# A decode convolution buffer with time outermost, and a decode z projection from the block in SBUF

## The chip, the cores and the metric

The kernel runs on one core of one Trainium2 chip. The metric is the device time of one execution in microseconds (us); it is the median of several runs. A profile is one more execution, taken by the hardware profiler; its span runs from the first to the last instruction.

## What is computed

The reference is one inference step of a one-layer hybrid trunk. A prompt of 2048 tokens and a decode batch of 8 sequences of 4 tokens (32 rows) share all weights. Each group goes through an input LayerNorm, a modulation of every channel by a vector `c`, one input projection, two mixers side by side (a state space branch and attention in a window of 128 with sinks), an output projection, a normalised residual, a squared-ReLU feed-forward part, and a second normalised residual. The state space branch is where the change lies:

```python
def causal_conv(u, buf, w, b):
    t = u.shape[1]
    up = jnp.concatenate([buf.astype(u.dtype), u], 1)
    y = up[:, 0:t] * w[0]
    for j in range(1, CONV_W):
        y = y + up[:, j:j + t] * w[j]
    return jax.nn.silu(y + b), up[:, t:]
...
    z = p[..., :Z_END]
    xbc = p[..., Z_END:XBC_END]
...
    y = y.reshape(b, t, SSM_WIDTH) * jax.nn.silu(z.astype(jnp.float32))
```

For the decode rows `buf` is `state_conv`, the last three positions of 1024 channels of each of the 8 sequences; the new state, the last three of the seven positions, is an output. The convolution has four taps. `z`, 512 channels, gates the branch's output.

## The kernel before

Everything is float32. A matmul whose operands must be exact is done as three: both operands are split into a high and a low part (`float32r`), and high x high, high x low and low x high are summed in PSUM (`mm3`, lines 164 to 167). The 32 decode rows have a cheaper way, `mm_dec` (lines 149 to 155): the high and low parts of the 32 rows stand side by side as 64 stationary columns, two matmuls for each block of 128 channels make 64 rows of partial sums in PSUM, ScalarE copies these to SBUF, and `sum2` (lines 157 and 158) adds the upper and the lower 32 rows by a matmul with a matrix of ones and zeros.

The work runs in sweeps. Sweep 1 makes step sizes, q, k, v and the attention of 16 token tiles of 128 and one decode tile, and stores the modulated input, split and transposed, in DRAM (`hT_d`). Sweep 2, which the change touches, goes over the tokens in 8 blocks of 256 (the loop at line 948). Block `BD` = 2 carries the decode tile as well, as columns 256 to 288 of its `hT`. For each block:

- `ld_hT` (line 632) brings in a block of `hT`, one block ahead. Even blocks use the buffers `hTa0` and `hTa1`, of which there is one each, so block 4's four loads (line 643) can only start when block 2's `hT` has been read for the last time. At block 2 two more loads (line 646) bring in the decode columns, high and low.
- `xproj` (line 654) makes the 8 groups of 128 convolution channels: 24 matmuls each into one of three PSUM tiles `mm`, an eviction by ScalarE (line 673), the convolution on VectorE (`conv4`, line 649: one instruction of line 650 and three of line 652), and a SiLU on ScalarE (line 679). At block 2 each group has 32 more columns, which VectorE copies from PSUM into the decode buffer `xd` (line 677) and convolves in the same way (line 678).
- `zproj` (line 826) makes `z` of a token tile; `zproj(2, 2)` makes that of the decode rows, by `mm_dec` and `sum2`. It loads its operand `hz` (line 833) from `hT_d` and puts `hz` and the copied partial sums into the rings of the tiles `X` and `Xd`.
- `ssd1` and `ssd2` (lines 844 and 904) do the scan of one chunk of 128 tokens. `ssd1` loads the running sums of the decays, broadcast to all partitions (`csb`, line 849), turns them into a masked decay matrix (VectorE line 863, ScalarE line 864, VectorE line 875), and makes `X` (line 865) and, on GpSimd, `Xd` (line 867). `ssd2` has PE's lines 913, 917 and 923, ends in VectorE's line 938, and stores its result to `yn_d` (line 939). `dec_half` does the decode part with the stored states.

The decode buffer `xd` is one SBUF tile. Its state part is loaded at the start of sweep 2 (line 822), and its last three positions are stored after `zproj(2, 2)` (line 969):

```python
xd = p2.tile([128, 8, 8, 7], F32, name="xd")
D.dma_start(out=xd[:, :, :, 0:3], in_=I["sconv"])
...
D.dma_start(out=O["convs"], in_=xd[:, :, :, 4:7])
```

The dimensions are channel in its group (partition), group, sequence, time. The DRAM sides, `sconv` and `convs`, have 192 contiguous values for each partition.

In this part of the kernel the order of the instructions on each engine comes from the compiler's scheduler: each engine runs its own list in order, and program order is the priority. Loads and stores named `D` are issued by SyncE (SP), one after the other, on one DMA queue; a DMA that has to wait for its buffer holds up those behind it on SP.

After sweep 2 come the output projection with the first residual (line 999 on) and the feed-forward part (from line 1197), which takes more than half of the time. Neither is touched.

Of the kernel before, what the change touches and what calls it, by code (L numbers as in the profile page):

```python
# [10 lines left out]
F32 = mybir.dt.float32  # L11
F32R = mybir.dt.float32r
# [8 lines left out]
ND = NB * NT_  # L21
NTOK = T + ND
DM, DFF = 1024, 4096
NTILE = T // 128
# [47 lines left out]
def host_arrays(i):  # L72
    a = {}
    f = lambda n: np.asarray(i[n])
    a["consts"], a["dmask"] = host_consts()
    a["x"] = np.concatenate([f("x_prompt")[0], f("x_sample").reshape(ND, DM)], 0)
    c = np.concatenate([f("c_prompt"), f("c_sample")], 0)
    a["cT"] = c.T.reshape(8, 128, 9).transpose(1, 0, 2)
    wa = f("w_ada")[0].reshape(8, 128, 6144)
    wc = wa[:, :, :2048].reshape(2, 4, 128, 2, 8, 128)[:, :, :, ::-1].transpose(4, 0, 2, 1, 3, 5)  # L80
    a["w_ac"] = wc.reshape(8, 2, 128, 1024)
    a["w_ada"] = wa[:, :, 2048:].reshape(8, 128, 8, 512).transpose(2, 1, 0, 3)
    col = lambda v: v.reshape(-1, 128).T
    a["acol"] = np.concatenate([col(f("b_ada")[0, :2048]), col(f("ln_in_g")), col(f("ln_in_b"))], 1)
    a["b_ada"] = f("b_ada")
    w = f("w_in")[0].reshape(8, 128, 2312)
    a["w1"] = w[:, :, 1536:2312]
    a["wx"] = w[:, :, 512:1536]
    a["wz"] = w[:, :, 0:512]
    cw = f("conv_w")[0].reshape(4, 8, 128).transpose(2, 1, 0)  # L90
    cb = f("conv_b")[0].reshape(8, 128).T[:, :, None]
    a["conv"] = np.concatenate([cw, cb], 2)
    a["sconv"] = f("state_conv")[0].reshape(8, 3, 8, 128).transpose(3, 2, 0, 1)
    h = 4 * np.arange(2)[:, None] + np.array(HR)[None, :]
    a["small"] = np.concatenate(
        [f("dt_bias"), f("A_log"), f("D_skip"), f("sinks")[:, h.reshape(-1)],
         f("sinks")], 0)
    a["normw"] = f("ssm_norm_w")
    a["rows"] = np.stack([f("ln_in_g"), f("ln_in_b"), f("ln1_g")[0], f("ln1_b")[0], f("ln2_g")[0], f("ln2_b")[0]], 0)
    wo = f("w_out")[0]  # L100
    att = wo[512:].reshape(2, 4, 64, 1024)[:, HR].transpose(1, 0, 2, 3).reshape(4, 128, 1024)
    a["wo"] = np.concatenate([wo[:512].reshape(4, 128, 1024), att], 0)
    a["wu"] = f("w_up")[0].reshape(8, 128, 32, 128).transpose(2, 1, 0, 3)
    a["wd"] = f("w_down")[0].reshape(32, 128, 1024)
    a["h0"] = f("state_ssm")[0].reshape(8, 512, 128).transpose(0, 2, 1)
    ck, cv = f("cache_k")[0], f("cache_v")[0]
    a["ckT"] = ck.transpose(3, 2, 0, 1).reshape(64, 2, 1024)
    a["ck"] = ck.reshape(8, 128, 128)
    a["cv"] = cv.reshape(8, 128, 128)
    return {k: np.ascontiguousarray(v) for k, v in a.items()}  # L110
# [1 line left out]

OUTS = {
    "y": (NTOK, DM), "convp": (128, 8, 3), "ssmp": (128, 512), "kp": (128, 128), "vp": (128, 128),
    "convs": (128, 8, 8, 3), "ssms": (8, 128, 512), "ks": (8, 128, 128), "vs": (8, 128, 128),
}


def body(tc, I, O):
    nc = tc.nc  # L120
    V, S, G, PE, D = nc.vector, nc.scalar, nc.gpsimd, nc.tensor, nc.sync
# [23 lines left out]
    ud_d = tc.dram_tile([2 * ND, DM], F32, name="ud_d")  # L145
    h2_d = tc.dram_tile([9, 128, 2, 8, 128], F32, name="h2_d")

# [1 line left out]
    def mm_dec(tmp, w, hs, wt):  # L149
        acc = mm_tile()  # L150
        for k in range(8):
            for l in range(2):
                PE.matmul(acc[:2 * ND, :w], lhsT=hs(k), rhs=wt(k, l), start=k + l == 0, stop=k + l == 8)
        S.activation(tmp[:2 * ND, :w], acc[:2 * ND, :w], AF.Copy)
        return tmp

    def sum2(out, tmp, w):
        PE.matmul(out[:ND, :w], lhsT=idt[:2 * ND, 192:224], rhs=tmp[:2 * ND, :w], start=True, stop=True)
# [5 lines left out]
    def mm3(out, ahi, alo, bhi, blo, first=True, last=True):  # L164
        PE.matmul(out, lhsT=ahi, rhs=bhi, start=first, stop=False)  # L165
        PE.matmul(out, lhsT=ahi, rhs=blo, start=False, stop=False)  # L166
        PE.matmul(out, lhsT=alo, rhs=bhi, start=False, stop=last)  # L167
# [18 lines left out]
    def ptok(t):  # L186
        return 128 if t < NTILE else ND

# [1 line left out]
    cp = pool("const")  # L190
    mhalf = cp.tile([128, 2], F32, name="mhalf")
    V.memset(mhalf, -0.5)
# [18 lines left out]
    dt_all = cs_.tile([128, NC, 8], F32, name="dt_all")  # L211
    V.memset(dt_all, 0.0)

# [1 line left out]
    pk = pool("dk")  # L215
    dk = {}
    for nm in ("cs", "ecs", "dst", "etot"):
# [58 lines left out]
        if ch < 7:  # L276
            ada_ld(ch + 1)

# [1 line left out]
    p1 = pool("sweep1")  # L280
    W1h = [page(k)[:, 0:776] for k in range(8)]
    W1l = [page(8 + k)[:, 0:776] for k in range(8)]
# [252 lines left out]
            D.dma_start(out=att_d[NTILE][:, :, :32], in_=ao)  # L535
            dec["p"].release()

# [1 line left out]
    def decays_a():  # L539
        cs, ecs, dst, etot = dk["cs"], dk["ecs"], dk["dst"], dk["etot"]  # L540
        bc = lambda a: a.unsqueeze(1).to_broadcast([128, NC, 8])
# [51 lines left out]
        D.dma_start(out=cs_d[0:128, :], in_=cT_[:, 0:128])  # L593
        D.dma_start(out=cs_d[128:136, 0:32], in_=cT_[:8, 128:160])

# [1 line left out]
    NA = 4  # L597
    Wx, Wz = {}, {}
    w2 = {}
# [49 lines left out]
    def conv4(dst_, src, f):  # L649
        V.tensor_scalar(dst_, src(0), cvw[:, f, 0:1], cvw[:, f, 4:5], ALU.mult, ALU.add)  # L650
        for j in range(1, 4):
            V.scalar_tensor_tensor(dst_, src(j), cvw[:, f, j:j + 1], dst_, ALU.mult, ALU.add)  # L652

    def xproj(b, fs):
        N = 256 if b != BD else 288
        hT = blk["hT", b]
        if fs[0] == 0:
            p, tg = (pb, "xcb") if b % 2 else (pb, "xca")
            blk["xc", b] = p.tile([128, 8, 256 if b % 2 else 288], F32, tag=tg, name="xc")
            blk["halo", b] = xq[:, 800 + 24 * (b % 2):824 + 24 * (b % 2)].rearrange("p (f t) -> p f t", t=3)  # L660
        xc, halo = blk["xc", b], blk["halo", b]
        for f in fs:
            o = 260 * ((8 * b + f) % 3)
            xp = xq[:, o:o + 259]
            if b == 0:
                V.memset(xp[:, 0:3], 0.0)
            else:
                V.tensor_copy(xp[:, 0:3], blk["halo", b - 1][:, f, :])
            mm = mm_tile()
            cs4 = slice(128 * f, 128 * f + 128)  # L670
            for k in range(8):
                mm3(mm[:, :N], Wx[k][0][:, cs4], Wx[k][1][:, cs4], hT[0][:, k, :N], hT[1][:, k, :N], k == 0, k == 7)
            S.activation(xp[:, 3:259], mm[:, 0:256], AF.Copy)
            V.tensor_copy(halo[:, f, :], xp[:, 256:259])
            conv4(xc[:, f, 0:256], lambda j: xp[:, j:j + 256], f)
            if N > 256:
                V.tensor_copy(xd[:, f, :, 3:7], mm[:, 256:288].rearrange("p (b t) -> p b t", b=8))
                conv4(xc[:, f, 256:288].rearrange("p (b t) -> p b t", b=8), lambda j: xd[:, f, :, j:j + 4], f)
            S.activation(xc[:, f, :N], xc[:, f, :N], AF.Silu)

    extras = [] + [lambda ch=ch: ada_step(ch) for ch in range(8)]
# [69 lines left out]
    for i in range(n + 3):  # L751
# [3 lines left out]
        t = g(i)  # L755
# [57 lines left out]
        extras.pop(0)()  # L813
    p1.release()

# [1 line left out]
    p2 = pool("sweep2")  # L817
    cs, ecs, dst, etot, etb = [dk[k] for k in ("cs", "ecs", "dst", "etot", "etb")]
    St = [p2.tile([128, 512], F32, name=f"St{j}") for j in range(2)]
    V.memset(St[0], 0.0)  # L820
    xd = p2.tile([128, 8, 8, 7], F32, name="xd")
    D.dma_start(out=xd[:, :, :, 0:3], in_=I["sconv"])
    hbc = lambda a, P: a.unsqueeze(2).to_broadcast([P, 8, 64])
    h3 = lambda a: a.rearrange("p (h d) -> p h d", h=8)

    def zproj(b, m):
        P = 128 if m < 2 else 32
        hT = blk["hT", b]
        mm = mm_tile()
        sl = slice(128 * m, 128 * m + P)  # L830
        if m == 2:
            hz = p2.tile([128, 8, 2 * ND], F32R, tag="X", name="hz", bufs=2)
            D.dma_start(out=hz.bitcast(F32), in_=hT_d[NTILE][:, 0, :, :2 * ND])
            tmp = mm_dec(p2.tile([128, 512], F32, tag="Xd", name="tmp", bufs=2), 512, lambda k: hz[:, k, :],
                         lambda k, l: Wz[k][l])
            sum2(mm, tmp, 512)
        else:
            for k in range(8):
                mm3(mm[:P, :], hT[0][:, k, sl], hT[1][:, k, sl], Wz[k][0], Wz[k][1], k == 0, k == 7)
        z = p2.tile([128, 512], F32, tag="z", name="z", bufs=3)  # L840
        S.activation(z[:P], mm[:P, :], AF.Silu)
        blk["z", 2 * b + m if m < 2 else NTILE] = z
# [105 lines left out]
    for b in range(7):  # L948
        ld_hT(b + 1)
        if b > 0:  # L950
            xproj(b, range(0, 4))
        if b > 0:
            ssd2(2 * b - 2)
            ssd1(2 * b - 1)
        if b == BD + 1:
            ssd1(NTILE)
        if b > 0:
            xproj(b, range(4, 8))
            ssd2(2 * b - 1)
        if b == BD + 1:  # L960
            dec_half(0)
        zproj(b, 0)
        ssd1(2 * b)
        if b == BD + 1:
            dec_half(1)
        zproj(b, 1)
        if b == BD:
            zproj(b, 2)
            D.dma_start(out=O["convs"], in_=xd[:, :, :, 4:7])
        if b == BD + 1:  # L970
            ssd2(NTILE)
    xproj(7, range(0, 4))
# [23 lines left out]
    S.dma_start(out=O["convp"], in_=blk["halo", 7])  # L996
    S.dma_start(out=O["ssmp"], in_=St[NTILE % 2])

# [1 line left out]
    first2 = {}  # L1000

    def q2(nm, dt_=F32):
# [191 lines left out]
    pw.release()  # L1194
    out_c(NTILE - 1)

# [1 line left out]
    p4 = pool("ffn")  # L1198
    T4 = {"st": (3, F32), "st2": (1, F32), "wvh": (1, F32R), "wvl": (1, F32R),
          "r": (2, F32), "gf": (1, F32), "wdh": (3, F32R), "wdl": (3, F32R)}  # L1200
# [329 lines left out]
```

## Time and profile before

| | |
|---|---|
| runs | 2547.44, 2553.53, 2552.56 us; median 2552.56 us |
| span of the profiled execution | 2549.4 us, 32193 instructions |
| mean granted PE clock | 0.976 |
| PE matmul busy | 2429.9 us (95%) |
| VectorE (DVE) busy | 1502.2 us (59%) |
| ScalarE (ACT) busy | 717.9 us (28%) |
| GpSimd (POOL) busy | 933.2 us (37%) |
| DMA | 133672 packets, 244.46 MB; 43408 packets under 512 B |

A row of a timeline is start, duration (us), engine, line of the kernel, operation, tile written <- tiles read, shapes and how many were merged; in brackets stands how long the engine had been idle before it, and what released it. SPq rows are DMA issues by SyncE: their duration is the time to issue, not to transfer. A row of waits is engine, tile and line, what it waited for, and then the total in us, the number of times and the longest. A row of windows is a stretch, its length, busy time of PE, PE's weight loads, DVE, ACT and POOL (with numbers of instructions), the granted PE clock, the mean busy share of the 16 DMA engines, and GB/s. Rows of a tile are number, minimum/median/maximum duration in ns, first and last start, and shapes.

### The profile page before, as it was taken

The numbers are of one execution on the slowest core, as the hardware profiler recorded it, in microseconds if no ns is written. First come the engines' busy times: TensorE is split into PE (matmuls) and PEld (weight loads), VectorE is DVE, ScalarE is ACT, GpSimd is POOL, SyncE is SP. The second block draws the span as 40 slices with busy tenths as digits, with TensorE's granted clock in tenths as the row PEclk, the third lists the DMA queues.
The fourth block names the chain that finished last, engine by engine and source line by source line (L and its number), as shares of the span: only waits on it lengthen the run. The fifth ranks groups of instructions, "written<-read, shape, count | busy, mean of one in ns | idle before, by whom it ended". The sixth has DMA issues, their size and how long they took to land.

```text
span 2549.4 us, 32193 instructions
## 1 busy us (share of the span) xinstructions
PE 2429.9 (95%) x12688; PEld 2013.2 (79%) x12688; DVE 1502.2 (59%) x2582; ACT 717.9 (28%) x1433; POOL 933.2 (37%) x602
## 2 busy tenths in 40 slices
PE   8999998959999998899999999999899999999997
PEld 6667787947997877687888888888788988988985
DVE  6756666837879888764544434447844344344347
ACT  3544474312434222312212121212221221221221
POOL 4323431213323454544333233435532332332335
PEclk9999999979999999999999999999899999999998
DMA  8644433483225435621111111117311110110111
GB/s 319 247 172 158 133 106 90 64 55 109 83 67 194 141 116 192 217 62 60 60 42 58 46 58 42 51 49 205 121 44 48 34 67 34 42 58 34 42 43 72
DMA packets 133672, 244.46 MB, mean 96 GB/s; under 512 B 43408, under 2 KB 78416, under 8 KB 130368
## 3 DMA queue, kind: packets, MB, share of 16 engines
q1 hardware_dynamic: 129120, 232.42, 29.5%
q10 hardware_dynamic: 4400, 9.98, 1.1%
q8 instruction: 100, 1.64, 0.3%
q14 instruction: 52, 0.43, 0.1%
HBM read 188.00 MB, written 55.37 MB: 95 GB/s over the span
## 4 chain that ended last, share of the span: by engine, by line
PE 52%; DVE 3%; issue 1%; POOL 1%; ACT 0%; POOLq 0%; DVEq 0%
PE sc L165 10%; PE sc L167 10%; PE sc L166 10%; PE mm L165 5%; PE mm L167 5%; PE mm L166 5%; PE tr L167 2%; PE tr L166 2%; PE tr L165 2%; PE tr L1282 1%; DVE p L1237 1%; DVE p L1294 0%; DVE nb L1306 0%; POOL rs L173 0%; DVE p L1313 0%
## 5 line engine op out<-in xcount | busy, mean ns | idle before, releaser
L162 POOL TENSOR_TENSOR wdl<-st,wdh 128x1024 fp32r<-128x1024 f32 x63 | 164.2, 2606 | 533.1 <-ACT wdh L161 533.1
L1267 DVE TENSOR_TENSOR r<-r 128x320 f32<-128x320 f32 (+1 forms) x160 | 148.4, 928 | 300.7 <-ACT u L1263 101.2
L1294 DVE TENSOR_TENSOR p<-mm,p 128x512 f32<-128x512 f32 x298 | 202.6, 686 | 175.6 <-PE mm L167 175.5
L161 ACT ACTIVATE wdh<-st 128x1024 fp32r<-128x1024 f32 x63 | 66.8, 1060 | 628.7 <-PE mm L167 244.9
L165 PE MATMUL sc<-H,wvh 128*128 128x352 f32 (+1 forms) x640 | 227.7, 356 | 5.9 <-ACT r L1261 5.9
L167 PE MATMUL sc<-H,wvl 128*128 128x352 f32 (+1 forms) x640 | 226.6, 354 | 0.0
L166 PE MATMUL sc<-H,wvh 128*128 128x352 f32 (+1 forms) x640 | 226.3, 354 | 0.0
L165 PE MATMUL sc<-H,wuh 128*128 128x352 f32 (+1 forms) x640 | 224.7, 351 | 0.0
L167 PE MATMUL sc<-H,wul 128*128 128x352 f32 (+1 forms) x640 | 224.0, 350 | 0.0
L166 PE MATMUL sc<-H,wuh 128*128 128x352 f32 (+1 forms) x640 | 223.9, 350 | 0.0
L1261 ACT ACTIVATE r<-sc 128x352 f32<-128x352 f32 (+1 forms) x160 | 81.7, 511 | 273.8 <-PE sc L167 237.0
L165 PEld LDWEIGHTS sc<-H,wvh 128*128 128x128 f32 x640 | 121.3, 189 | 18.8 <-ACT r L1261 6.2
L166 PEld LDWEIGHTS sc<-H,wvh 128*128 128x128 f32 x640 | 121.2, 189 | 12.0
L167 PEld LDWEIGHTS sc<-H,wvl 128*128 128x128 f32 x640 | 120.8, 189 | 12.2
L165 PEld LDWEIGHTS sc<-H,wuh 128*128 128x128 f32 x640 | 120.5, 188 | 11.5 <-ACT r L1261 0.8
L167 PEld LDWEIGHTS sc<-H,wul 128*128 128x128 f32 x640 | 121.0, 189 | 10.5
L166 PEld LDWEIGHTS sc<-H,wuh 128*128 128x128 f32 x640 | 120.7, 189 | 10.2
L173 POOL TENSOR_TENSOR rs<-ve,mhalf 128x1 f32<-128x1 f32 (+2 forms) x68 | 48.6, 715 | 207.7 <-DVE ve L172 186.2
L1143 DVE TENSOR_TENSOR st<-st,gf 128x1024 f32<-128x1024 f32 x64 | 84.7, 1323 | 56.3 <-POOL wdl L162 46.9
L1294 DVE TENSOR_TENSOR p<-tr,p 128x512 f32<-128x512 f32 x102 | 69.8, 687 | 75.3 <-PE tr L167 75.3
L1266 DVE TENSOR_TENSOR ud<-r 128x32 f32<-128x32 f32 x32 | 58.3, 1822 | 94.8 <-ACT r L1261 94.8
L652 DVE SCALAR_TENSOR_TENSOR xc<-xq,cvw,xc 128x256 f32<-128x256 f32 x192 | 103.2, 541 | 2.8
(487 smaller groups left out, 6635.2 us busy)
## 6 DMA issues: line engine op xcount, KB each, us to landing
st<-in_wd SPq DMA_DIRECT2D x64, 512.0 KB
st<-in_wu SPq DMA_DIRECT2D x63, 512.0 KB
wa<-in_w_ada SPq DMA_DIRECT2D x32, 512.0 KB
hT_d<-hb SPq DMA_DIRECT2D x16, 1024.0 KB
hT<-hT_d SPq DMA_DIRECT2D x16, 512.0 KB
hT<-hT_d SPq DMA_DIRECT2D x8, 1024.0 KB
csb<-cs_d SPq DMA_DIRECT2D x16, 512.0 KB
p<-xhat_d SPq DMA_DIRECT2D x16, 512.0 KB
```

The costliest lines, as they stand in the source:

```text
L161: S.activation(hi, src, AF.Copy)
L162: (eng or V).tensor_tensor(lo, src, hi.bitcast(F32), ALU.subtract)
L165: PE.matmul(out, lhsT=ahi, rhs=bhi, start=first, stop=False)
L166: PE.matmul(out, lhsT=ahi, rhs=blo, start=False, stop=False)
L167: PE.matmul(out, lhsT=alo, rhs=bhi, start=False, stop=last)
L173: G.tensor_tensor(r[:P], v[:P], mhalf[:P, 0:n], ALU.pow)
L652: V.scalar_tensor_tensor(dst_, src(j), cvw[:, f, j:j + 1], dst_, ALU.mult, ALU.add)
L1143: V.tensor_tensor(st, raw, scale, ALU.mult)
L1261: S.activation(r[:, :n], mm[:, :n], AF.Relu)
L1266: V.tensor_tensor(ud, r[:, w:n], r[:, w:n], ALU.mult)
L1267: V.tensor_tensor(r[:, :w], r[:, :w], r[:, :w], ALU.mult)
L1294: V.tensor_tensor(acc[t][:, sl], mm, acc[t][:, sl], ALU.add)
```

## The change

The decode buffer `xd` is laid out as partition, time, group, sequence, and the DRAM arrays `sconv` and `convs` with it. So the state part is the first 3 x 64 values of each partition and the new state the last 3 x 64: both are contiguous on both sides. The host's arrangement of input and output changes to match. VectorE's copy from PSUM and its convolution get views in which time stands before sequence. `zproj(2, 2)` no longer loads `hz` and no longer uses `mm_dec` and `sum2`; it is done like the others, with `mm3`, from columns 256 to 288 of the block's `hT` in SBUF, 32 rows at a time. The rest of the diff is comments removed.

```diff
-    a["sconv"] = f("state_conv")[0].reshape(8, 3, 8, 128).transpose(3, 2, 0, 1)
+    a["sconv"] = f("state_conv")[0].reshape(8, 3, 8, 128).transpose(3, 1, 2, 0)
...
-    "convs": (128, 8, 8, 3), "ssms": (8, 128, 512), "ks": (8, 128, 128), "vs": (8, 128, 128),
+    "convs": (128, 3, 8, 8), "ssms": (8, 128, 512), "ks": (8, 128, 128), "vs": (8, 128, 128),
...
-                V.tensor_copy(xd[:, f, :, 3:7], mm[:, 256:288].rearrange("p (b t) -> p b t", b=8))
-                conv4(xc[:, f, 256:288].rearrange("p (b t) -> p b t", b=8), lambda j: xd[:, f, :, j:j + 4], f)
+                tb = lambda a: a.rearrange("p (b t) -> p t b", b=8)
+                V.tensor_copy(xd[:, 3:7, f, :], tb(mm[:, 256:288]))
+                conv4(tb(xc[:, f, 256:288]), lambda j: xd[:, j:j + 4, f, :], f)
...
-    xd = p2.tile([128, 8, 8, 7], F32, name="xd")
-    D.dma_start(out=xd[:, :, :, 0:3], in_=I["sconv"])
+    xd = p2.tile([128, 7, 8, 8], F32, name="xd")
+    D.dma_start(out=xd[:, 0:3], in_=I["sconv"])
...
-        if m == 2:
-            hz = p2.tile([128, 8, 2 * ND], F32R, tag="X", name="hz", bufs=2)
-            D.dma_start(out=hz.bitcast(F32), in_=hT_d[NTILE][:, 0, :, :2 * ND])
-            tmp = mm_dec(p2.tile([128, 512], F32, tag="Xd", name="tmp", bufs=2), 512, lambda k: hz[:, k, :],
-                         lambda k, l: Wz[k][l])
-            sum2(mm, tmp, 512)
-        else:
-            for k in range(8):
-                mm3(mm[:P, :], hT[0][:, k, sl], hT[1][:, k, sl], Wz[k][0], Wz[k][1], k == 0, k == 7)
+        for k in range(8):
+            mm3(mm[:P, :], hT[0][:, k, sl], hT[1][:, k, sl], Wz[k][0], Wz[k][1], k == 0, k == 7)
...
-            D.dma_start(out=O["convs"], in_=xd[:, :, :, 4:7])
+            D.dma_start(out=O["convs"], in_=xd[:, 4:7])
...
-        np.ascontiguousarray(o["convs"].transpose(2, 3, 1, 0)).reshape(1, 8, 3, 1024),
+        np.ascontiguousarray(o["convs"].transpose(3, 1, 2, 0)).reshape(1, 8, 3, 1024),
```

## The prediction

> **What bounds the kernel now.** I read the page first, then the waits of TensorE (PE), then the timeline around the longest of them, then the DMA view of the same stretch. On the page PE is busy in nine tenths or more of nearly every slice:
>
> ```profile
> span 2549.4 us, 32193 instructions
> ...
> PE   8999998959999998899999999999899999999997
> ```
>
> So time can only be won where PE is made to stand still. Slice 9 (510 to 573 us) has a 5 in the middle of the state space sweep. The waits of PE between 400 and 700 us (engine, its line, what it waited for: total us, times, longest) name the cause:
>
> ```profile
> PE mm L153 <- DMA hz<-hT_d: 28.0, 1, 28.0
> PE sc L923 <- DVE csb L875: 1.8, 1, 1.8
> ...
> PE mm L165 <- ACT xq L673: 0.8, 1, 0.8
> ```
>
> One wait of 28.0 us is for the operand `hz` of the decode z projection, the second thing that the change touches. The timeline (start, duration, engine, line, what; in brackets the idle time before it and its releaser) shows that `hz` is not what is slow:
>
> ```profile
> 498.15 0.59 SPq L969 DMA_DIRECT2D out_convs<-xd  x1
> ...
> 498.88 21.80 SPq L849 DMA_DIRECT2D csb<-cs_d  x1
> ...
> 503.85 1.46 DVE L652 SCALAR_TENSOR_TENSOR xc<-xd,cvw,xc 128x32 f32<-128x32 f32 x2
> ...
> 511.51 1.02 PE L913 MATMUL sc<-St,xc 128*128 128x256 f32 x4
> 520.73 2.20 SPq L833 DMA_DIRECT2D hz<-hT_d  x1
> 539.65 1.66 DVE L863 TENSOR_SCALAR csb<-csb,dk_cs 128x128 f32<-128x128 f32 x8 [34.34 <-DMA csb<-cs_d]
> ...
> 540.56 5.68 PE L153 MATMUL mm<-pg,hz 128*64 128x512 f32 x16 [28.02 <-DMA hz<-hT_d]
> ...
> 542.13 1.05 POOL L867 TENSOR_TENSOR Xd<-X,dk_dst 128x512 f32<-128x512 f32 x1
> ...
> 543.77 1.28 DVE L875 TENSOR_TENSOR csb<-csb,cbm 128x512 f32<-128x512 f32 x2
> 543.91 0.32 SPq L939 DMA_DIRECT2D yn_d<-y  x1
> 544.33 4.92 SPq L643 DMA_DIRECT2D hT<-hT_d  x4
> ...
> 546.08 1.03 PE L917 MATMUL sc<-Xd,Bt 128*128 128x256 f32 x4
> ...
> 549.00 1.04 PE L158 MATMUL mm<-tmp,idt 64*32 64x512 f32 x2
> 549.41 1.32 SPq L849 DMA_DIRECT2D csb<-cs_d  x1
> ...
> 549.97 0.39 PE L165 MATMUL mm<-hT,Wx 128*128 128x256 f32 x1
> ```
>
> The convolution store is issued at 498.15; the next issue on SP, `csb`, then takes 21.80 us instead of a third of one, `hz` goes out only at 520.73, and both land together near 540. What runs in between is the store:
>
> ```profile
> DMA packets 7601, 0.10 MB, mean 4 GB/s; under 512 B 7600, under 2 KB 7600, under 8 KB 7600
> ```
>
> That is the DMA view from 498 to 522 us: 7600 packets, 0.10 MB. The old buffer has time innermost, seven places with three of them stored, so the 96 KB go out in 128 x 64 = 8192 pieces of 12 bytes. VectorE (DVE), ScalarE, GpSimd and PE all stand still behind it: DVE waited 34.34 us for `csb`, PE 28.02 us for `hz`.
>
> **The store and the z projection.** With the new layout the store is 128 pieces of 768 bytes. Its price is not in the trace; it lies between the 256 KB store `yn_d` just above (0.32 us to issue) and what it costs now. I take the lower end, since `yn_d` also is one contiguous run per partition. Then `csb` has the queue to itself from 498.9. The decode `csb` of 549.41, which stands behind four 512 KB loads, landed by 555.37 (row below), 6.0 us after its issue; so 504.9 is a late estimate. DVE is free of its convolution at 503.85 + 1.46 = 505.3, so it no longer waits. From L863 at 539.65 to the end of L875 at 543.77 + 1.28 it needed 5.4 us, to the end of `Xd` on GpSimd 3.5 us: in the new kernel 510.7 and 508.8.
>
> PE's side: `L913` starts at 511.51. Its group takes 0.87 us of issue, and a 512-column matmul of this stage 0.232 us, from these rows:
>
> ```profile
> 495.19 1.02 PE L913 MATMUL sc<-St,xc 128*128 128x256 f32 x4
> ...
> 496.06 1.03 PE L917 MATMUL sc<-Xd,Bt 128*128 128x256 f32 x4
> ```
>
> ```profile
> 508.03 0.39 PE L165 MATMUL mm<-pg,hT 128*128 128x512 f32 x1
> ...
> 510.12 0.39 PE L165 MATMUL mm<-pg,hT 128*128 128x512 f32 x1
> ```
>
> (nine starts in 2.09 us). The new decode z has 24 such matmuls (three products, eight blocks) in place of 16. Only their stationary side is narrower (32 columns); I charge full pace, 24 x 0.232 = 5.6 us. So PE comes to L917 at 511.51 + 0.87 + 5.57 = 517.95 instead of 546.08: **28.1 us won**, and the operands (508.8, 510.7) are there. If `csb` came later than about 512 this cover would be gone and PE would wait for it at L917, one for one.
>
> The two summing matmuls L158 go as well; PE's next starts 549.97 - 549.00 = **1.0 us** earlier. ScalarE's copy before them and the load of `hz` cost nothing today beyond the stall and win nothing.
>
> **The load.** The old state load has the same 12-byte pieces, in SBUF, and it too blocks `csb`:
>
> ```profile
> 420.51 1.86 SPq L822 DMA_DIRECT2D xd<-in_sconv  x1
> ...
> 422.47 6.77 SPq L849 DMA_DIRECT2D csb<-cs_d  x1
> ...
> 429.49 0.16 DVE L668 COPY xq<-xq 128x3 f32<-128x3 f32 x1
> ...
> 433.59 1.66 DVE L863 TENSOR_SCALAR csb<-csb,dk_cs 128x128 f32<-128x128 f32 x8 [3.94 <-DMA csb<-cs_d]
> ...
> 439.74 2.00 PE L923 MATMUL sc<-X,csb 128*128 128x64 f32 x16 [1.79 <-DVE csb L875]
> ```
>
> ```profile
> GB/s 290 273 200 232 268 318 317 324 331 328 316 329 328 338 300 273 101 69 53 41 33 32 29 25 23 21 17 11 5 4 3 2 42 123 191 314 218 137 232 191
> ```
>
> The last row cuts 420 to 432 us into 0.3 us slices: 15 to 16 of them, some 4.6 us, move almost nothing. Without them `csb` lands at about 429.0, before DVE is free at 429.65; DVE starts 3.94 us earlier, and PE's wait of 1.79 us at L923, which hangs on that DVE chain, should go. Behind that wait the granted clock (before-last group: clock, DMA share, GB/s) sank:
>
> ```profile
> 440.00:445.00 5.00, 5.00 (x34) 5.00 (x34) 5.00 (x20) 2.69 (x3) 0.43 (x1) 0.71 0.33 123
> 445.00:450.00 5.00, 5.00 (x40) 4.92 (x39) 5.00 (x10) 1.71 (x8) 2.39 (x2) 0.95 0.00 0
> ```
>
> 0.29 x 5 and 0.05 x 5 of lost clock are 3.4 us at half speed, 1.7 us of work. I count both: **3.5 us won**.
>
> Here a rule of the Trainium skill speaks against me. "TensorE: Matmul & The Clock Gate", Part 1 (the HAM clock gate), says that the clock falls to half after an idle window of about 3.4 us. By it a wait of 1.79 us would not lower the clock, the 1.7 us would have another cause and might stay, and the sum would be 1.7 us smaller. The row has the low clock right behind the short wait, so I follow the row.
>
> **A wait that the change adds.** The decode z now reads block 2's `hT`. The four loads of L643 write block 4 into the same buffer, so they wait for its last matmul. Queued behind them on SP is the decode `csb` (L849), and for that DVE, then ScalarE, then PE wait already today:
>
> ```profile
> 555.37 1.25 DVE L863 TENSOR_SCALAR csb<-csb,dk_cs 32x32 f32<-32x32 f32 x8 [5.81 <-DMA csb<-cs_d]
> ...
> 556.69 1.28 ACT L864 ACT_TABLE_LOAD   x1 [6.03 <-DVE csb L863]
> ...
> 559.11 0.62 ACT L673 ACTIVATE xq<-mm 128x256 f32<-128x256 f32 x2
> ...
> 559.51 0.38 PE L165 MATMUL mm<-hT,Wx 128*128 128x256 f32 x1 [0.78 <-ACT xq L673]
> ```
>
> ScalarE cannot empty the PSUM tiles of the next `xproj` while it waits, and after three tiles PE stops (0.78 us). Today the loads go out at 544.33, 5.64 us before that `xproj` starts at 549.97. In the new kernel they go out when the last z matmul is done, 517.72 + 0.40 = 518.1, and `xproj` starts at 517.95 + (549.00 - 546.08) = 520.9: a lead of 2.8 us. The decode `csb` comes 2.9 us later for PE, the wait grows from 0.8 to 3.7 us: **2.9 us lost**, and as much clock as behind the first wait, **1.7 us**. Bounds: nothing, if the compiler's order changes, and 4.6 us.
>
> **DVE.** Its 40 small instructions per kernel now read and write permuted views; today:
>
> ```profile
> L652 DVE SCALAR_TENSOR_TENSOR xc<-xd,cvw,xc x24: 235/243/1190, 470.4 to 504.1; 128x32 f32<-128x32 f32 x24
> L677 DVE COPY xd<-mm x8: 175/181/189, 469.3 to 497.9; 128x32 f32<-128x32 f32 x8
> L650 DVE TENSOR_SCALAR xc<-xd,cvw x8: 291/294/299, 469.8 to 499.2; 128x32 f32<-128x32 f32 x8
> ```
>
> They already step over groups of seven, so I take no change; the bounds are a few hundredths of a us less each and the 1.19 us maximum.
>
> **Sum.** -28.1 - 1.0 - 3.5 + 2.9 + 1.7 = -28.0 us. On the profiled span: 2549.4 - 28.0 = 2521.4. The median of the runs, 2552.56, lies 3.2 us above that span; I keep this distance: **2524.6 us**. After 560 us PE is full and nothing in the other stages is touched, so I carry the gain to the end.
>
> **Rivals.** 0.3% is 7.7 us, about what a measurement of this kernel can tell from no change.
> A, no new wait: the order on SP or ScalarE changes with the instructions, and the decode `csb` is not behind the loads. -32.6, 2520.0 us. For it: the order comes out of a scheduler; against: the loads stand ahead of that `csb` today, and nothing in the diff speaks to their order.
> B, the low clock at 442 us is not that wait's doing and stays: -26.3, 2526.3 us. Against it: the place in the trace. For it: the wait is short beside the 28 us one.
> C, the first wait stays whole, since the DVE chain from 429 on is full and something else in it is late: -24.5, 2528.1 us.
> D, the change does not do what it says: the contiguous store blocks the queue as long, and the wait for `hz` becomes one for `csb`. `Xd` would be done at 543.2 as now, L917 would follow at 543.3 and `xproj` at 546.2, 3.8 us earlier; but the loads of L643 (544.33, behind `yn_d`) would lead it by only 1.9 us, and PE would give these 3.8 us back at ScalarE. 2552.6 us. Against it: 4 GB/s in 12-byte pieces.
> E, slower: the permuted DVE instructions each take the 1.19 us maximum. 24 x 0.95 + 8 x 0.90 + 8 x 1.01 = 38 us on a DVE that was 5.00 of 5 us busy in the convolution of this block, whose end PE's L858 awaits: -28 + 38, 2562.6 us. It decides from 28/40 = 0.7 us more per instruction. Against it: the maximum is one outlier, the median 0.243 us.
>
> **Chances.** Forecast 0.45, A 0.25, B 0.13, C 0.10, D 0.04, E 0.03. Range: A to C, and the scatter of the runs before about their median (-5.1, +1.0), with one more clock window of 1.7 us at the top: 2515 to 2531. Faster 0.93, same 0.04, slower 0.03.
>
> **What would show it.** Right: no wait of PE over 5 us between 500 and 560; the issue of `csb` behind the store at a third of a us; no `hz`, no L158 there, 24 matmuls with 32 stationary columns; DVE not waiting at 429; a PE wait for ScalarE L673 of 3 to 4 us some 8 us after the z, with a dip of the clock. Wrong: a long wait for `csb`, small DVE instructions near 1 us, or a PE gap of over 2 us near 434.

## The result and the profile after

| | before | after |
|---|---|---|
| median of the runs beside each other | 2553.05 us (2547.44 to 2553.82, 4 runs) | 2522.98 us (2521.64 to 2524.95, 4 runs) |
| span of the profiled execution | 2549.4 us | 2520.5 us |

The ratio is 0.9889 with a 95% interval of 0.9877 to 0.9901: 1.1% faster. The forecast was 2524.6 us in a range of 2515 to 2531. The span fell by 2549.4 - 2520.5 = 28.9 us, where the sum had 28.0. The total is right; two of the steps under it are not, and in this pair of traces they nearly cancel.

The page of the kernel after:

```profile
span 2520.5 us, 32205 instructions
...
PE   7899999999998988899999999999999999999997
...
DMA packets 116504, 244.19 MB, mean 97 GB/s; under 512 B 25984, under 2 KB 61248, under 8 KB 113200
```

The 5 in the ninth place of PE's row is a 9. Of the packets under 512 bytes, 43408 - 25984 = 17424 are gone; two transfers of 8192 pieces make 16384 of these. The waits of PE in the kernel after, 400 to 700 us, are all that is left there:

```profile
PE sc L852 <- ACT xc L680: 2.9, 4, 0.8
PE sc L852 <- DVE yt L920: 0.4, 1, 0.4
```

From `zproj` on, a line of the kernel before stands six lines earlier in the kernel after: L849, L863 and L913 are L843, L857 and L907. The issues on SP in the kernel after:

```profile
496.09 0.34 SPq L963 DMA_DIRECT2D out_convs<-xd  x1
496.62 0.64 SPq L843 DMA_DIRECT2D csb<-cs_d  x1
...
515.00 4.19 SPq L643 DMA_DIRECT2D hT<-hT_d  x4
530.09 0.34 SPq L843 DMA_DIRECT2D csb<-cs_d  x1
```

The first two lines answer to the store and the 21.80 us issue of before: `csb` now goes out in 0.64 us. The last two are a surprise, to which the text comes back: the decode `csb`, which stood right behind the four loads, now goes out 530.09 - 519.19 = 10.9 us after them, with SP idle in between. PE in the same stretch:

```profile
509.53 0.39 PE L165 MATMUL mm<-pg,hT 128*32 128x512 f32 x1
...
514.81 0.39 PE L167 MATMUL mm<-pg,hT 128*32 128x512 f32 x1
...
526.40 1.03 PE L907 MATMUL sc<-St,xc 128*128 128x256 f32 x4
```

The 24 matmuls of the decode z run from 509.53 to 514.81 at 5.28/23 = 0.230 us each: the full pace that was charged, though the stationary side is 32 columns. No wait stands before or behind them. VectorE in the kernel after:

```profile
427.72 1.66 DVE L857 TENSOR_SCALAR csb<-csb,dk_cs 128x128 f32<-128x128 f32 x8 [2.03 <-DMA csb<-cs_d]
...
503.25 1.65 DVE L857 TENSOR_SCALAR csb<-csb,dk_cs 128x128 f32<-128x128 f32 x8
```

At 427.72 it still waits for `csb`, 2.03 us in place of 3.94, and 5.9 us earlier than before; at 503.25 it finds `csb` there, where it had waited 34.34 us.

Where the time was won and given back shows when the same row is found in both traces. PE's first row of block 3's first chunk before, and after:

```profile
576.56 1.02 PE L913 MATMUL sc<-St,xc 128*128 128x256 f32 x4
```

```profile
543.38 1.03 PE L907 MATMUL sc<-St,xc 128*128 128x256 f32 x4
```

SP's first load of the output projection's weights, its last store of `xhat` (the end of that stage), and its last store of all, before and after:

```profile
771.31 4.12 SPq L984 DMA_DIRECT2D p<-in_wo  x8
...
1214.68 0.32 SPq L1373 DMA_DIRECT2D xhat_d<-g  x1
...
2544.66 2.20 SPq L1499 DMA_DIRECT2D out_y<-p  x4
```

```profile
739.39 4.45 SPq L978 DMA_DIRECT2D p<-in_wo  x8
...
1187.15 0.32 SPq L1367 DMA_DIRECT2D xhat_d<-g  x1
...
2515.69 2.20 SPq L1493 DMA_DIRECT2D out_y<-p  x4
```

The gain is 33.2 us at block 3, 31.9 at the end of sweep 2, 27.5 at the end of the output projection and 29.0 at the end. So sweep 2 won about 4 us more than the sum, and a stage that the change does not touch gave as much back.

### The profile page after: what moved, and what is told of

Read it like the earlier page. It is cut to its first block, busy times and chain, and to the rows that moved or that the text cites. A ratio compares the mean times of both kernels' runs of the same rounds, so it can differ in the third digit from the quotient of the medians.

```text
span 2520.5 us, 32205 instructions
## 1 busy us (share of the span) xinstructions
PE 2421.1 (96%) x12694; PEld 2004.7 (80%) x12694; DVE 1510.5 (60%) x2582; ACT 720.2 (29%) x1434; POOL 930.8 (37%) x602
## 2 busy tenths in 40 slices
DMA packets 116504, 244.19 MB, mean 97 GB/s; under 512 B 25984, under 2 KB 61248, under 8 KB 113200
## 4 chain that ended last, share of the span: by engine, by line
PE 53%; DVE 3%; POOL 1%; issue 1%; DMA 0%; ACT 0%; SPq 0%; POOLq 0%; DVEq 0%; ACTq 0%
PE sc L165 10%; PE sc L167 10%; PE sc L166 10%; PE mm L165 5%; PE mm L167 5%; PE mm L166 5%; PE tr L165 2%; PE tr L167 2%; PE tr L166 2%; PE tr L1276 1%; DVE p L1231 1%; DVE nb L1300 0%; DVE p L1232 0%; POOL rs L173 0%; DVE p L1307 0%
## 5 line engine op out<-in xcount | busy, mean ns | idle before, releaser
L165 PE MATMUL sc<-H,wvh 128*128 128x352 f32 (+1 forms) x640 | 227.1, 355 | 5.3 <-ACT r L1255 5.3
L165 PE MATMUL sc<-H,wuh 128*128 128x352 f32 (+1 forms) x640 | 224.4, 351 | 0.0
L165 PEld LDWEIGHTS sc<-H,wvh 128*128 128x128 f32 x640 | 120.8, 189 | 18.3 <-ACT r L1255 5.7
L165 PEld LDWEIGHTS sc<-H,wuh 128*128 128x128 f32 x640 | 120.4, 188 | 11.4 <-ACT r L1255 0.8
```

## The experiments

The theory: the store in 12-byte pieces alone makes the stall; the load is worth a few us; the new z is worth nothing by itself. The rivals: that the new z, which does without `hz`, is what removes the stall; that only SP's queue is held and not the transfers; and, for why the store is slow, the number of its pieces, their size or where they lie. Ratios are to the kernel before on the same chip.

**The layout alone.** As after, but with the decode z of before (`hz`, `mm_dec`, `sum2`):

```diff
-    xd = p2.tile([128, 8, 8, 7], F32, name="xd")
-    D.dma_start(out=xd[:, :, :, 0:3], in_=I["sconv"])
+    xd = p2.tile([128, 7, 8, 8], F32, name="xd")
+    D.dma_start(out=xd[:, 0:3], in_=I["sconv"])
...
-            D.dma_start(out=O["convs"], in_=xd[:, :, :, 4:7])
+            D.dma_start(out=O["convs"], in_=xd[:, 4:7])
```

> The kernel before with the new buffer layout alone; the decode z keeps its own operand load, its 16 matmuls and the two summing matmuls. Theory (the store of 12-byte pieces is the cause): both long waits go, 28 to 33 us faster, ratio 0.987 to 0.989, the operand's load lands within 6 us of its issue and PE never waits over 3 us between 490 and 550 us. PE has about 0.9 us less to do than in the changed kernel, so at most 1 us from it either way. Rival (the separate load of the decode z operand is the cause): the wait of PE for it stays at 20 us or more and only the first wait goes, 3.5 us, ratio 0.9985.

2519.82 us, ratio 0.9884 (0.9861 to 0.9906). Its issues on SP:

```profile
495.80 0.34 SPq L970 DMA_DIRECT2D out_convs<-xd  x1
496.32 0.62 SPq L850 DMA_DIRECT2D csb<-cs_d  x1
496.99 0.43 SPq L834 DMA_DIRECT2D hz<-hT_d  x1
```

`hz` is still loaded, and goes out in time: PE has no wait for it. The whole gain comes with the layout.

**After, once more**, on the same chip: the kernel after, not edited.

> The changed kernel once more, for the scatter between executions and for a second trace. Ratio 0.988 to 0.990. If the output projection gives back 4 us of the gain as a rule, the stretch from the first load of the output weights to the first store of the last feed-forward input is 4 us longer than in the kernel before here too; if that was scatter, it differs from the first trace of the same kernel by 2 us or more.

2523.47 us (the kernel before: 2548.58), 0.9903 (0.9885 to 0.9921), just outside the expected 0.988 to 0.990. The interval overlaps that of the layout alone, so these runs do not tell the two apart. The stretch of the output projection, which was the second question, is taken up below.

**The store alone.** The load and z as before; VectorE copies the new state into a contiguous tile, which is stored:

```diff
-            D.dma_start(out=O["convs"], in_=xd[:, :, :, 4:7])
+            xs = p2.tile([128, 8, 32], F32, tag="cm", name="xs").rearrange("p b t -> p (b t)")[:, 0:192]
+            xs = xs.rearrange("p (f b t) -> p f b t", f=8, b=8)
+            V.tensor_copy(xs, xd[:, :, :, 4:7])
+            D.dma_start(out=O["convs"], in_=xs)
```

> The kernel before; VectorE copies the last three positions into a contiguous tile and the store goes from there (128 pieces), the load stays as it was, and the decode z too. Theory: the wait of 28 us at the decode z goes and that of 1.8 us near 438 us, with its low clock, stays: 26 to 30 us faster, ratio 0.988 to 0.990. Rival (the operand load of the decode z): under 4 us.

2521.33 us, 0.9892 (0.9876 to 0.9909). Of PE's waits of before, the one which belongs to the load stays; that for `hz` is gone, and no other of over 0.9 us has come between 400 and 700 us:

```profile
PE sc L923 <- DVE csb L875: 1.8, 1, 1.8
```

**The new z alone**, on the old layout:

```diff
-        if m == 2:
-            hz = p2.tile([128, 8, 2 * ND], F32R, tag="X", name="hz", bufs=2)
...
-            sum2(mm, tmp, 512)
-        else:
-            for k in range(8):
-                mm3(mm[:P, :], hT[0][:, k, sl], hT[1][:, k, sl], Wz[k][0], Wz[k][1], k == 0, k == 7)
+        for k in range(8):
+            mm3(mm[:P, :], hT[0][:, k, sl], hT[1][:, k, sl], Wz[k][0], Wz[k][1], k == 0, k == 7)
```

> The kernel before with the new decode z alone; the store and load keep their 12-byte pieces. Theory: the stall stays, as a wait for the decays of the next chunk instead of for the z operand: ScalarE cannot evict the three PSUM tiles before those decays land near 540 us, so PE stops from about 518 to 544 us; within 4 us of before, ratio 0.9985 to 1.0015. Rival (the operand load of the decode z is the cause): 25 us or more faster, ratio 0.990.

2548.04 us, 0.9998 (0.9987 to 1.0009): nothing. Its issue of `csb` behind the store takes 20.75 us, and PE does its z and then stands still all the same:

```profile
PE mm L165 <- ACT z L834: 21.8, 1, 21.8
```

ScalarE's eviction of z (L834) is the releaser that the trace names; ScalarE stands behind VectorE, whose longest wait there is 31.8 us for `csb`. With `hz` gone, the other operand behind the same store takes its place. That refutes the rival.

**The load alone**, staged through a contiguous tile:

```diff
-    D.dma_start(out=xd[:, :, :, 0:3], in_=I["sconv"])
+    xl = p2.tile([128, 256], F32, tag="h0", name="xl", bufs=6)[:, 0:192].rearrange("p (f b t) -> p f b t", f=8, b=8)
+    D.dma_start(out=xl, in_=I["sconv"])
+    V.tensor_copy(xd[:, :, :, 0:3], xl)
```

> The kernel before; the state load goes into a contiguous tile (128 pieces), from which VectorE copies it into the old buffer; the store stays in 12-byte pieces. Theory: the wait of 1.8 us near 438 us and the 3.4 us of low clock behind it go, the 28 us stay: 2 to 4 us faster, ratio 0.9984 to 0.9992. If the low clock there is not that wait's doing, it is still in the trace and the gain is 2 us or less.

2546.31 us, 0.9991 (0.9982 to 1.0000): about 2 us, in an interval that ends at no change. PE's wait at L923 is gone, the clock behind that place is 1.00, and the wait for `hz` stays at 25.2 us.

**The same store from ScalarE's queue:**

```diff
-            D.dma_start(out=O["convs"], in_=xd[:, :, :, 4:7])
+            S.dma_start(out=O["convs"], in_=xd[:, :, :, 4:7])
```

> The kernel before with the same store of 12-byte pieces issued by ScalarE, on its own DMA queue, instead of SyncE. If the store hurts because later loads stand behind it in one queue, the loads of the decays and of the z operand pass it and the wait goes nearly whole: 24 to 28 us faster, ratio 0.989 to 0.991. If the 12-byte writes hold the DMA engines themselves, whatever queue they come from, the wait stays at 15 us or more and the gain is under 12 us, ratio over 0.995.

2544.56 us, 0.9983 (0.9974 to 0.9992). SP is free at once, and the hold-up moves to the next large transfer:

```profile
499.53 0.43 SPq L833 DMA_DIRECT2D hz<-hT_d  x1
...
514.53 27.60 SPq L643 DMA_DIRECT2D hT<-hT_d  x4
542.30 1.26 SPq L849 DMA_DIRECT2D csb<-cs_d  x1
```

```profile
PE mm L165 <- ACT xq L673: 12.4, 1, 12.4
PE mm L153 <- DMA hz<-hT_d: 7.9, 1, 7.9
```

`hz` went out 21.2 us earlier than before and PE still waits 7.9 us for it; the four loads take 27.60 us to issue. So another queue does not get round the store: the transfers themselves are held, as the second of the two expected outcomes had it. This agrees with the Trainium skill, "DMA: Bandwidth & Descriptors", section "Issuing engines are not separate DMA queues", by which transfers run on the same 16 engines whoever issued them. The run also shows the wait that the prediction had feared: the decode `csb` behind the four loads, then ScalarE, then PE at L165, 12.4 us.

**96-byte pieces.** As after, with time as the middle dimension, so that both transfers are 1024 pieces of 96 bytes:

```diff
-    xd = p2.tile([128, 7, 8, 8], F32, name="xd")
-    D.dma_start(out=xd[:, 0:3], in_=I["sconv"])
+    xd = p2.tile([128, 8, 7, 8], F32, name="xd")
+    D.dma_start(out=xd[:, :, 0:3], in_=I["sconv"])
...
-            D.dma_start(out=O["convs"], in_=xd[:, 4:7])
+            D.dma_start(out=O["convs"], in_=xd[:, :, 4:7])
```

> The changed kernel with time as the middle dimension (group, time, sequence): load and store in 1024 pieces of 96 bytes instead of 128 of 768. If the cost goes with the number of pieces, the store takes an eighth of 40 us, about 5 us, which the convolution still hides: within 2 us of the changed kernel, ratio 0.988 to 0.990. If every piece under 512 bytes is slow by more than its number says, the wait for the decays is back, 5 us or more, ratio over 0.991.

2522.62 us, 0.9896 (0.9883 to 0.9910), like the kernel after. The DMA view from 497 to 500 us, in slices of 0.075 us:

```profile
GB/s 0 0 0 218 0 0 0 0 0 0 0 0 0 0 0 0 0 0 0 0 0 0 0 0 0 0 0 0 0 14 110 152 132 129 132 132 136 127 126 317
DMA packets 1021, 0.13 MB, mean 43 GB/s; under 512 B 1016, under 2 KB 1016, under 8 KB 1020
```

The store takes ten slices, 0.8 us, at some 130 GB/s, where 5 us were expected from an eighth of the pieces. So the cost does not go with the number of pieces alone, and a piece need not be long.

**Both transfers staged**, old layout and old z: the two edits with `xs` and `xl` together.

> The kernel before with contiguous load and store through two staging tiles; layout of the buffer, convolution and decode z as before. Theory: as good as the changed kernel, 28 to 33 us faster, ratio 0.987 to 0.989. If the new views cost VectorE anything, this is faster than the layout alone by the same amount; I expect no difference over 1 us.

2518.73 us, 0.9884 (0.9869 to 0.9900). PE has no wait over 0.9 us between 400 and 700 us. Two copies on VectorE do what the new layout does.

**12-byte pieces, one to a stretch of 512 bytes.** The kernel before; the strided store goes to an extra scratch array in DRAM, and the real output follows from `xs`, so this kernel has one store more:

```diff
+    cv_d = tc.dram_tile([128, 64, 128], F32, name="cv_d")
...
-            D.dma_start(out=O["convs"], in_=xd[:, :, :, 4:7])
+            D.dma_start(out=cv_d[:, :, 0:3].rearrange("p (f b) t -> p f b t", f=8), in_=xd[:, :, :, 4:7])
...
+            V.tensor_copy(xs, xd[:, :, :, 4:7])
+            D.dma_start(out=O["convs"], in_=xs)
```

> The kernel before with two stores of the last three positions: the same 8192 pieces of 12 bytes as before, but into a scratch array in which each piece has 512 bytes to itself, and behind it a contiguous one (through a copied tile) into the output. If the pieces are slow because neighbours in DRAM touch the same few bytes' line, the store now takes about as long as the load of 8192 pieces did, under 10 us, and the wait of PE for the z operand is under 5 us: 2518 to 2526 us. If each short write is slow by itself, it takes some 27 us as before and PE waits 20 us or more: 2545 to 2553 us.

2527.49 us in one run (the kernel before beside it: 2551.62), 1.5 us above the expected range. SP's issues:

```profile
497.71 0.57 SPq L970 DMA_DIRECT2D cv_d<-xd  x1
499.24 6.00 SPq L974 DMA_DIRECT2D out_convs<-xs  x1
```

**The same with a stretch of 16 bytes:** `cv_d` is [128, 64, 4].

> The same with 16 bytes for each piece: every piece is aligned to 16 bytes, but neighbours still lie close together. If closeness in DRAM is the cause, PE waits 20 us or more for the z operand, 2545 to 2553 us. If only the odd alignment of 12-byte pieces is, it is as quick as with 512 bytes, 2518 to 2526 us.

2547.47 us in one run, and SP's issues:

```profile
498.18 0.57 SPq L970 DMA_DIRECT2D cv_d<-xd  x1
499.71 18.34 SPq L974 DMA_DIRECT2D out_convs<-xs  x1
```

The same number of pieces of the same size: the issue behind them takes 6.00 us where they lie 512 bytes apart, and 18.34 us where they lie 16 bytes apart. PE's wait for `hz` is 1.9 us in the one, 21.5 us in the other. So with the number and the size of the pieces kept, it is the distance between neighbours that makes the store slow; and a start on a multiple of 16 bytes does not help. The run with 512 bytes has one more wait, which the expectation did not have:

```profile
PE mm L166 <- ACT xq L674: 2.2, 1, 2.2
```

It is the wait that the prediction had added, and the text comes back to it.

**32-byte pieces.** The kernel after with an output in the order group, time, sequence, stored position by position:

```diff
-            D.dma_start(out=O["convs"], in_=xd[:, 4:7])
+            for t in range(3):
+                D.dma_start(out=O["convs"][:, :, t, :], in_=xd[:, 4 + t])
```

> The changed kernel with the output arranged as group, time, sequence and stored by three DMAs, one for each position, in 3072 pieces of 32 bytes; the load stays contiguous. By the number of pieces alone (1024 pieces of 96 bytes took under 1 us) it takes 3 us and is hidden: no PE wait over 3 us between 490 and 550 us, 2518 to 2526 us. If close short writes are slow, 3072 of them take some 10 us, and the decays of the next chunk come later than 505 us.

2524.47 us in one run. The DMA view from 496 to 502 us, in slices of 0.15 us:

```profile
GB/s 109 0 0 0 0 0 0 0 0 0 0 0 0 23 58 54 54 29 37 55 55 53 18 102 52 51 54 175 139 273 55 300 328 273 410 382 218 273 164 218
DMA packets 3246, 0.60 MB, mean 100 GB/s; under 512 B 3127, under 2 KB 3127, under 8 KB 3244
```

3072 pieces go out from slice 14 on at about 50 GB/s, in 2.3 us by their records, and `csb` behind them takes 0.60 us to issue. They are not held. The three stores together fill DRAM without gaps, but this does not make the pieces as close as before: within one store they start 96 bytes apart (three positions of eight values), the gaps being filled by the other two stores. So the run does not part the size of a piece from its distance. Over all runs, stores with starts 12 and 16 bytes apart take 3.2 to 3.3 ns for each piece, and those with starts 96 bytes (pieces of 32 and of 96) and 512 bytes apart 0.7 to 1.1 ns. If it is the distance alone, the border lies between 16 and 96 bytes; 12-byte pieces at a distance in between were not tried, and what sets the border the runs do not show.

**Before, once more**, not edited, for the scatter of the stall and of the output projection:

> The kernel before once more, for a second trace: from the first load of the output weights to the last store of the residual in the feed-forward part it took 443.4 us in the first trace, the changed kernel 447.8 and 447.9 us. If the 4 us that the changed kernel gave back there are its own, this trace is within 1 us of 443.4; if it is scatter between executions, it lies elsewhere between 440 and 450 us. The wait of PE for the z operand is 25 to 30 us, and the clock is low for one window near 442 us.

2548.87 us; span 2547.0 us. The wait for `hz` is 24.5 us here, not 28.0, and just under the expected 25 to 30; the clock is low behind the first wait again, 0.66 in the window from 440 to 445 us:

```profile
PE mm L153 <- DMA hz<-hT_d: 24.5, 1, 24.5
```

So the stall itself varies by some us from one execution to the next.

## Why the prediction was right, and where it was not

**The store (-28.1): right.** The store alone gives the whole gain within the intervals, the z alone 0.9998. By the first trace the gain grew from 495.19 - 492.94 = 2.3 us (PE's L913 and L907 of block 2) to 33.2 us at block 3, 30.9 us in between; the sum had 28.1 + 1.0 there. Of the rest, 0.8 us is the old wait at L673, which went too; about 1 us I do not place. `csb`, which was to be there by 504.9, was there by 503.25 at the latest.

One reading under this step was too short: not all of the time up to 540 us is the store's own. By the records of the packets its last piece ends at 526.2 in the kernel before; what then takes until 539.3 is the load of `csb` behind it. The DMA view of the kernel before from 528 to 544 us, in slices of 0.4 us:

```profile
GB/s 10 0 31 41 51 10 20 20 41 20 41 31 31 20 10 10 31 10 10 20 10 10 10 10 10 123 326 288 266 139 15 0 0 0 0 0 0 0 0 0
```

For 10 us the 512 KB of `csb` come at 51 GB/s or less; then `hz` comes at up to 326. In the kernel after the packets of the same load take 2.4 us, from 497.9 to 500.3; before, 16.4 us, from 522.9 to 539.3. So a slow store also slows the load behind it, for some 13 us after its last piece. Why is not shown.

**The two L158 matmuls (-1.0), with the new z.** They are gone; the z is 24 matmuls at the pace charged. In the kernel with the layout alone, which has no stall, the old form shows its true price:

```profile
509.34 4.05 PE L153 MATMUL mm<-pg,hz 128*64 128x512 f32 x16
...
516.14 1.04 PE L158 MATMUL mm<-tmp,idt 64*32 64x512 f32 x2
```

The 16 matmuls take 4.05 us (5.68 us in the kernel before, where the clock of the window from 540 to 545 us is 0.55); the 24 new ones, by the rows above, 514.81 + 0.39 - 509.53 = 5.67. The z edit thus costs PE 1.6 us there and saves the 1.0 us of L158: about nothing, and the run with the new z alone shows nothing.

**The first wait (-3.5): right in size.** PE reaches its next L913 at 449.28 before, and in the kernel after:

```profile
446.03 1.03 PE L907 MATMUL sc<-St,xc 128*128 128x256 f32 x4
```

That is 3.3 us, and 0.5 us of it is older than the change: SP's store of L593 stood at 416.75 before and stands at 416.22 after. VectorE was expected not to wait for `csb`; it waits 2.03 us, since it comes to it at 425.69 and not at 429.65, but PE does not wait for it. About 1 us of this gain is gone again by 492.94; 0.7 us of it is one of PE's waits for ScalarE L680, which before has none between those rows.

The clock went as the row had it, against the rule that was weighed. The windows from 440 to 450 us of the kernel after:

```profile
440.00:445.00 5.00, 5.00 (x45) 5.00 (x44) 5.00 (x12) 1.30 (x5) 2.46 (x2) 1.00 0.00 0
445.00:450.00 5.00, 5.00 (x37) 4.72 (x36) 4.40 (x18) 4.27 (x5) 0.87 (x1) 1.00 0.00 0
```

0.71 and 0.95 are 1.00. Rival B is refuted.

**The new wait (+2.9) and its clock (+1.7): wrong.** This is the step that failed. No wait of PE for L673 is left. The prediction took it that the scheduler would keep its order: z, then `xproj` of block 3 with the decode `csb` right behind the loads. In the kernel after it puts `ssd2` of block 2's second chunk after four groups of `xproj` (PE's L907 at 526.40) and issues the decode `csb` only at 530.09. That is rival A's condition, which had 0.25, and sweep 2 ended 31.9 us earlier, by A's -32.6. A's text said that nothing in the diff speaks to that order. The traces say that the new z does: in all five traces with it, one of them on the old layout, the decode `csb` goes out 9.9 to 11.0 us after the loads; in the nine with the old z it follows them within 3.4 us. From the run with the new z alone:

```profile
541.88 4.97 SPq L643 DMA_DIRECT2D hT<-hT_d  x4
556.73 0.34 SPq L842 DMA_DIRECT2D csb<-cs_d  x1
```

That the loads can lead to such a wait is shown by the run with the store on ScalarE's queue (12.4 us). How long it would have been with the new z in the old order was not tried, but the run with 512 bytes comes near it. There the loads, in the old order, lead `xproj` by 521.68 - 517.76 = 3.9 us, and PE waits 2.2 us for ScalarE, with a clock of 0.85 and 0.80 in the two windows of 5 us from 530; in the kernel before the lead was 5.64 us and the wait 0.78. So 1.7 us less lead made 1.4 us more wait: the cost and the clock were about rightly sized for the old order, and it is the order that was wrong.

**"I carry the gain to the end": wrong in this pair of traces.** 4.4 us are given back in the output projection. The instructions of each engine stand in the same order there before and after, so it is no new order. The length from the first load of `wo` to the last store of `xhat` is 1214.68 - 771.31 = 443.4 us before and 1187.15 - 739.39 = 447.8 after; in the repeats 446.3 for the kernel before and 447.9 for the kernel after, with the layout alone 440.5, with the z alone, which is no faster, 449.7. So the stage varies by up to 9 us among kernels with the same work there, in no order that follows the gain. There is one that follows the z: the five traces with the new z have 446.9 to 449.7 us, the nine with the old one 440.5 to 446.7. The ratios lean the same way: 0.9884 twice with the old z and both transfers mended, 0.9889, 0.9896 and 0.9903 with the new, in intervals that overlap. Whether the new z lengthens this stage, by some 3 us, was not tried, and what sets its length in an execution stays open. The medians of the first comparison differ by 2553.05 - 2522.98 = 30.1 us, those of the repeat by 2548.58 - 2523.47 = 25.1: that the span hit the sum to within 1 us is partly luck, the 25 to 30 us are not.

**DVE (0): nearly right.** The small instructions of the kernel after, by tile:

```profile
L652 DVE SCALAR_TENSOR_TENSOR xc<-xd,cvw,xc x24: 260/272/1184, 468.1 to 502.1; 128x32 f32<-128x32 f32 x24
L678 DVE COPY xd<-mm x8: 179/182/186, 467.0 to 495.9; 128x32 f32<-128x32 f32 x8
L650 DVE TENSOR_SCALAR xc<-xd,cvw x8: 304/310/315, 467.5 to 497.2; 128x32 f32<-128x32 f32 x8
```

The medians rise by 29, 1 and 16 ns: 24 x 0.029 + 8 x 0.001 + 8 x 0.016 = 0.8 us in all. ScalarE's L680 follows the convolution on DVE, and PE follows L680 in the four waits shown above (2.9 us); whether the slower instructions are behind these waits was not tried. The 1.18 us maximum is one outlier as before; rival E is refuted, and so are C and D, whose waits did not come.

## What to carry to other kernels

When an engine waits long for a small load, look at what stands ahead of that load on its queue, and at the GB/s row of that stretch: here the load of the late operand was not the cause, and taking it away moved the wait to the next one behind the same store. Before a layout is changed for a transfer, a staged copy on an engine with room tells in three lines what the transfer costs, and may be all that is needed. Where a scheduler sets the order, a wait that follows from today's order is a rival and not a term of the sum.

## What the runs showed of the hardware

- **12-byte stores close together are slow, the same load is not.** By the records of their packets, from the first start to the last end, 96 KB in 8192 pieces of 12 bytes took 26.8 us to write side by side (25.8 in the second trace), 26.5 us at 16 bytes' distance and 8.7 us at 512; 5.5 us in the load; 3072 pieces of 32 bytes, 96 apart, took 2.3 us and 1024 of 96 bytes 0.8 us. All of these pieces are under 512 bytes, so the count of small packets on the page does not tell them apart.
- **A held transfer holds those of other queues.** With the store on ScalarE's queue, SP's four loads took 27.60 us to issue, where they take 4.19 us in the kernel after.
- **A wait of under 2 us of PE can be followed by half clock, and its length alone does not decide.** In all six traces with a wait of 1.8 to 2.0 us at PE's L923 near 440 us the clock in the window behind it was 0.66 to 0.73 (in the kernel before it is 0.50 from 442.5 to 445.0); in the trace with a wait of 1.6 us there, and in the seven with none or 0.2 us, it was 1.00. Elsewhere this does not hold. In the run with 512 bytes a wait of 1.92 us, which ends at 514.07, has no low clock behind it. In the run with the new z alone the clock sinks behind two shorter waits, of 1.3 and 0.8 us, which end at 648.76 and 650.30; in the run with 32-byte pieces it is 0.72 from 625 to 630, behind waits of 1.1 and 0.8 us. The windows of the first two:

```profile
510.00:515.00 5.00, 3.08 (x14) 2.08 (x13) 2.27 (x11) 1.37 (x2) 0.42 (x1) 1.00 0.58 131
515.00:520.00 5.00, 5.00 (x30) 3.76 (x28) 4.68 (x9) 3.45 (x4) 1.72 (x3) 1.00 0.32 91
```

```profile
645.00:650.00 5.00, 3.21 (x17) 2.15 (x16) 5.00 (x10) 0.59 (x2) 3.98 (x3) 1.00 0.14 54
650.00:655.00 5.00, 4.70 (x15) 3.87 (x16) 4.97 (x16) 4.51 (x8) 1.71 (x2) 0.66 0.02 9
```

What else decides stays open. The Trainium skill, "TensorE: Matmul & The Clock Gate", Part 1, has the clock fall after an idle window of about 3.4 us; here single waits of 1.8 to 2.0 us, and pairs of shorter ones, were followed by it, and one of 1.92 us was not.
